# Chunk inverses of a delta rule: doublings on 32-row diagonal blocks in place of 64-row blocks

## The chip, the core and the metric

One NeuronCore of a Trainium2 chip runs the whole program in one launch. Its engines work side by side, each through its own instructions in order: TensorE (PE) multiplies matrices from SBUF into PSUM, VectorE (DVE) and ScalarE (ACT) do elementwise work and read PSUM back, GpSimd (POOL) does a little, and SyncE (SP) issues most DMAs. The metric is the device time of one execution in microseconds; lower is better. Times of before are the median of three runs.

## The reference, cut to what matters

A small network on 256 tokens of width 1024: two mixed attention layers, then two layers of feed-forward, a mixing layer, and feed-forward again. The change sits in the mixing layer, in its generalized delta rule of eight heads of 64:

```python
def rwkv7_scan(r, w, k, v, a, b):
    def step(state, inp):
        r_t, w_t, k_t, v_t, a_t, b_t = inp
        sa = jnp.einsum('bhvk,bhk->bhv', state, a_t)
        state = (state * w_t[:, :, None, :] + sa[..., None] * b_t[:, :, None, :]
                 + v_t[..., None] * k_t[:, :, None, :])
        return state, jnp.einsum('bhvk,bhk->bhv', state, r_t)
    ...
    _, y = lax.scan(step, state0, xs)
```

Written in chunks of 64 tokens, the steps inside a chunk are a triangular system of 64 unknowns for each head and chunk. The kernel inverts its unit triangular matrix, and the change is in how.

## The kernel before

**Stages.** `network` runs `even`, `odd`, and then twice `ffn`, `mix`, `ffn`. Weights come from HBM as one stream; SyncE loads parts of 128 x 1024 values, ACT casts each to a high part (`whi`, line 117), DVE subtracts for a low part (`wlo`, line 118), and each projection step is three matmuls of 128 x 128 weights on 256 columns (`mm3`, lines 131 to 133; in `proj_n` lines 317 to 319). `fetch_to` runs four parts ahead of the one in use.

**The mixing layer.** `mix` has two units of four heads. For each it makes k, r and v (`project`), `operands`, and `chunks`; then `chain` walks both units over the four chunks, and `retention` follows. The functions are generators, but alone in `together` a generator's yields change nothing. What sets the order on every engine is a scheduler over the whole program, which places an instruction by its estimate of when its inputs are there; so the projection matmuls of unit 1 and of the retention stand between the steps of `chunks`.

**`chunks`.** A unit has 16 matrices of 64 x 64: two heads on the two halves of the 128 partitions, eight (head pair and chunk) along the free axis. The gram matmuls (line 992) give, masked by `gm`, `gb` and `gk`. The inverse of the unit triangular matrix in `gb[:, :, 0:64]` is built by doubling: `xT` starts with the inverse of blocks of two (lines 998, 999, masks `lev[:, 0]` and `eye`), `x` is its transpose (line 1000; DVE's stream transpose works in blocks of 32 x 32). Level s joins blocks of 2^s to blocks of 2^(s+1):

```python
ps = pairs("t1", lambda e, p, n: gb[p, n, 0:64], lambda e, p, n: x[p, n])
nc.vector.tensor_tensor(t1, ps, b8(lev[:, s]), op=OP.mult)
...
ps = pairs("dx", lambda e, p, n: xT[p, n], lambda e, p, n: t1[p, n])
nc.vector.tensor_tensor(x, ps, x, op=OP.add)
nc.vector.transpose(flat(xT), flat(x))
```

`pairs` (line 975) is 16 matmuls of 64 rows by 64 columns, one for each matrix; the two heads lie on different halves of the array. There are five levels, so ten products in a call; the last adds to `xT` itself (line 1044). Beside them run `values` (vt, line 1009 and 1012), `updates` (bt and nbk, lines 1018 and 1021) and `first` (z, line 975 and 1027). `chain` reads `xT` in its u matmuls (line 1068). Two PSUM banks (`inv`) take turns. In the trace the PSUM tile t1 and the SBUF tile t1 are both named "t", and each program matmul of 32-bit operands of this kind gives two records.

Of the kernel before, what the change touches and what calls it, by code (L numbers as in the profile page):

```python
# [9 lines left out]
F32 = mybir.dt.float32  # L10
# [3 lines left out]
OP = mybir.AluOpType  # L14
# [37 lines left out]
class Net:  # L52
# [782 lines left out]
    def mix(self, tag, l, cst):  # L835


        nc, tc, ident = self.nc, self.tc, self.ident
# [3 lines left out]
        with ExitStack() as c:  # L842
            psum = self.banks.using(mm=(0, 1), ch=(2, 4), ss=(3,), inv=(5, 6), y=(7, 3))
            work = c.enter_context(tc.tile_pool(name="mw", bufs=1))

            gm, lev, eye, scan, rot, cos, sin, dec = (cst[n] for n in MIX_CONST)
# [72 lines left out]
            def w8(name, n, bufs=2):  # L919
                return work.tile([128, 8, n], F32, tag=name, name=name, bufs=bufs)  # L920

            c8 = lambda t: t.rearrange("p u (c t) -> p (u c) t", t=C)
            flat = lambda m: m.rearrange("p n t -> p (n t)")
# [47 lines left out]
            def pairs(name, lhs, rhs, tag="inv"):  # L971
                ps = psum.tile([128, 8, 64], F32, tag=tag, name=name)
                for n in range(8):
                    for e, p in enumerate(heads):
                        nc.tensor.matmul(ps[p, n], lhs(e, p, n), rhs(e, p, n), start=True, stop=True)  # L975
                return ps

            def chunks(q, b):


                ar, bk, v = (q[n] for n in ("ar", "bk", "v"))

                gb, gk = w8("gb", 128), w8("gk", 128)
                for u in range(2):
                    yield
                    m = slice(4 * u, 4 * u + 4)
                    pb = psum.tile([128, 4, 128], F32, tag="inv", name="gram")
                    pk = psum.tile([128, 4, 128], F32, tag="inv", name="gram")
                    for n in range(4):
                        for ps, w in ((pb, heads[0]), (pk, heads[1])):  # L990
                            for p in heads:
                                nc.tensor.matmul(ps[p, n], bk[p, 4 * u + n, w], ar[p, 4 * u + n], start=True, stop=True)  # L992
                    for g, ps in ((gb, pb), (gk, pk)):
                        nc.vector.tensor_tensor(g[:, m], ps, gm[:, None, :].to_broadcast([128, 4, 128]), op=OP.mult)

                b8 = lambda m: m[:, None, :].to_broadcast([128, 8, 64])
                x, xT = w8("x", 64, 1), w8("xT", 64)
                nc.vector.tensor_tensor(xT, gb[:, :, 0:64], b8(lev[:, 0]), op=OP.mult)
                nc.vector.tensor_tensor(xT, xT, b8(eye), op=OP.add)
                nc.vector.transpose(flat(x), flat(xT))  # L1000

                vt = work.tile([128, 2, 4, 64], F32, tag="vt", name="vt", bufs=2)
                nbk = work.tile([128, 8, 2, 64], F32, tag="nbk", name="nbk", bufs=2)

                def values():
                    ps = psum.tile([128, 2, 2, 128], F32, tag="inv", name="vt")
                    for u in range(2):
                        for i in range(2):
                            nc.tensor.transpose(ps[:, u, i], v[:, u, 128 * i:128 * i + 128], ident)
                    for i, p in enumerate(heads):  # L1010
                        for e in range(2):
                            nc.scalar.copy(vt[heads[e], :, i::2], ps[p, :, :, heads[e]])

                def updates(u):
                    m = slice(4 * u, 4 * u + 4)
                    ps = psum.tile([128, 4, 128], F32, tag="inv", name="bt")
                    for n in range(4):
                        nc.tensor.transpose(ps[:, n], bk[:, 4 * u + n], ident)
                    for i in range(2):
                        for p in heads:  # L1020
                            nc.scalar.copy(nbk[p, m, i], ps[heads[i], :, p])

                def first():
                    ps = pairs("z0", lambda e, p, n: gk[p, n, 0:64],
                               lambda e, p, n: vt[p, n // 4, n % 4])
                    z0 = q["z0"] = work.tile([128, 2, 4, 64], F32, tag="z0", name="z0", bufs=2)
                    nc.scalar.copy(z0.rearrange("p u n t -> p (u n) t"), ps)

                side = [values, lambda: updates(0), lambda: updates(1), first]
                t1 = w8("t1", 64, 1)  # L1030
                for s in range(1, 6):
                    yield
                    ps = pairs("t1", lambda e, p, n: gb[p, n, 0:64], lambda e, p, n: x[p, n])
                    nc.vector.tensor_tensor(t1, ps, b8(lev[:, s]), op=OP.mult)
                    if side:
                        side.pop(0)()
                    yield
                    if s < 5:
                        ps = pairs("dx", lambda e, p, n: xT[p, n], lambda e, p, n: t1[p, n])
                        nc.vector.tensor_tensor(x, ps, x, op=OP.add)  # L1040
                        nc.vector.transpose(flat(xT), flat(x))
                    else:
                        ps = pairs("dx", lambda e, p, n: t1[p, n], lambda e, p, n: xT[p, n])
                        nc.vector.tensor_tensor(xT, ps, xT, op=OP.add)
                q.update(gb=gb, gk=gk, vt=vt, nbk=nbk, xT=xT)

            def chain(q, b):
# [92 lines left out]
            for name in "krv":  # L1140
                project(name, 0)
            together(operands(units[0], 0))
            together(chunks(units[0], 0))
            for name in "krv":
                project(name, 1)
# [274 lines left out]
def constants():  # L1420

    f = np.float32
    p = np.arange(128)
    c = {}
    c["ident"] = np.eye(128, dtype=f)
    c["e2"] = (p[:, None] // 64 == np.arange(2)[None]).astype(f)
    slopes = np.power(2.0, -np.arange(1, 9)).astype(f)
    t1, t0 = p[:, None] + 128, p[:, None]
    keys = np.concatenate([np.tile(np.arange(256), (128, 1)), np.tile(np.arange(128), (128, 1))], 1)
    dist = np.concatenate([np.tile(t1, 256), np.tile(t0, 128)], 1) - keys  # L1430
    c["dist"] = np.stack([np.where((dist >= 0) & (dist < w), dist, -NEG) for w in (256, 128)], 1).astype(f)
    pairs = [2.0 ** -(4 * e + t + 1) for t in range(4) for e in range(2)]
    sl = np.stack([1 / slopes, slopes, 1 / np.array(pairs), pairs])
    c["slopes"] = np.broadcast_to(sl[None], (128, 4, 8)).astype(f)
    c["blk64"] = (p[:, None] // 64 == p[None] // 64).astype(f)
    tp = p[:, None, None] + 128 * np.arange(2)[None, :, None]
    dc = (tp - (16 * np.arange(15) + 31)[None, None]).astype(f)
    c["cmask"] = (dc >= 0).astype(f)
    cb = np.where(dc[:, :, None] >= 0, -slopes[None, None, :, None] * dc[:, :, None], f(NEG))
    c["cbias"] = cb.astype(f).reshape(128, 16, 15)  # L1440

    s, t = p[:, None] % 64, p[None] % 64
    c["gm"] = np.where(p[None] < 64, s < t, s <= t).astype(f)
    s, t = p[:, None] % 64, np.arange(64)[None]
    lev = [(s // 2 == t // 2) & (s < t)]
    for w in (2, 4, 8, 16, 32):
        lev.append((s // (2 * w) == t // (2 * w)) & (s // w > t // w))
    c["lev"] = np.stack(lev, 1).astype(f)
    c["eye"] = (s == t).astype(f)
    c["scan"] = np.broadcast_to((np.arange(S) % 64 != 0).astype(f)[None], (128, S))  # L1450
    half = p % 64 // 32
    c["rot"] = np.zeros((128, 128), f)
    c["rot"][np.where(half == 0, p + 32, p - 32), p] = np.where(half == 0, f(-1), f(1))
    inv = (f(1.0) / np.power(f(10000.0), np.linspace(0.0, 1.0, 32, dtype=f))).astype(f)
    ang = (inv[p % 32][:, None] * np.arange(S, dtype=f)[None]).astype(f)
    c["cos"], c["sin"] = np.cos(ang).astype(f), np.sin(ang).astype(f)
    i, j = np.arange(S)[None], np.arange(S)[:, None]
    d = np.where(i // 64 == j // 64, np.abs(i - j), np.where(i > j, i - j, np.inf))
    lg = np.log(1.0 - np.power(2.0, -5.0 - np.arange(4)))
    dec = np.exp(lg[:, None, None] * d[None]) * 64 ** -0.5  # L1460
    c["dec"] = dec[:, :128].transpose(1, 0, 2).astype(f)
    c["vmask"] = ((p[:, None] // 15) == np.arange(8)[None]).astype(f)
    return c
# [54 lines left out]
```

## Time and profile before

| what | us |
|---|---|
| median of 3 runs (1466.73 to 1468.81) | 1468.05 |
| the profiled execution | 1467.17 |
| its span, first to last instruction | 1465.4 |
| PE busy (98%) | 1432.1 |
| DVE busy (69%) | 1013.0 |
| ACT busy (50%) | 739.8 |

The page gives each engine's busy time, the chain of work that ended last, and groups of instructions by line. A matmul's row gives its start and a modelled length in which neighbours overlap, so what a matmul costs is read from start to start. The mean granted TensorE clock is 0.991.

### The profile page before, as it was taken

Reading aid. Unit: us, or ns where it says so; the run is one execution under the profiler, and the core shown is the slowest. Engines: PE = TensorE matmul, PEld = TensorE weight load, DVE = VectorE, ACT = ScalarE, POOL = GpSimd, SP = SyncE. Lnnn points to the kernel's source line nnn. Section 1 sums busy time; section 2 is a strip of 40 time slices with the busy share of each in tenths; the row PEclk is TensorE's granted clock in tenths of the full one; section 3 lists DMA queues with packets and bytes.
Section 4 is the critical chain, followed back from the end, with each engine's and each line's share of the span. In section 5 each row is a group of like instructions: output and inputs, shape, how many; then the busy total and the mean of one; then the engine's idle time right before and its main releaser. Section 6 shows DMA issues by size and latency. Waiting matters only on the chain.

```text
span 1465.4 us, 31747 instructions
## 1 busy us (share of the span) xinstructions
PE 1432.1 (98%) x13326; PEld 1370.9 (94%) x13326; DVE 1013.0 (69%) x1804; ACT 739.8 (50%) x1268; POOL 23.9 (2%) x54
## 2 busy tenths in 40 slices
PE   8899989999999999999999999999999999999997
PEld 7699979899999989898999999999998988999997
DVE  7879798886555678657655668556678756765564
ACT  6947555855444474335444445444457324544443
POOL 0000000000000000000000000000000001000000
PEclk9999999999999999999999999999999999999998
DMA  8244534265555534124555555555553213555551
GB/s 297 76 130 132 179 125 144 87 206 177 186 184 184 180 116 129 47 87 122 180 181 182 187 187 173 184 178 187 187 173 116 74 32 101 173 178 183 186 187 44
DMA packets 63600, 222.01 MB, mean 151 GB/s; under 512 B 7744, under 2 KB 9024, under 8 KB 63456
## 3 DMA queue, kind: packets, MB, share of 16 engines
q1 hardware_dynamic: 62928, 219.31, 47.0%
q8 instruction: 104, 1.70, 0.5%
q10 hardware_dynamic: 432, 0.53, 0.1%
q14 instruction: 40, 0.33, 0.1%
q0 software_dynamic: 96, 0.13, 0.0%
HBM read 218.90 MB, written 1.05 MB: 150 GB/s over the span
## 4 chain that ended last, share of the span: by engine, by line
PE 91%; ACT 4%; DVE 3%; issue 1%; POOL 1%; DMA 0%; POOLq 0%; DVEq 0%; ACTq 0%
PE gu L131 11%; PE gu L133 11%; PE gu L132 11%; PE mm L132 6%; PE mm L131 6%; PE mm L133 6%; PE acc L131 6%; PE acc L132 6%; PE acc L133 6%; PE t L975 2%; PE dx L975 1%; PE gram L992 1%; PE gu L282 1%; PE s L370 1%; ACT whi L117 1%
## 5 line engine op out<-in xcount | busy, mean ns | idle before, releaser
L118 DVE TENSOR_TENSOR wlo<-raw,whi 128x1024 fp32r<-128x1024 f32 (+1 forms) x412 | 499.1, 1213 | 209.2 <-ACT whi L117 208.8
L117 ACT CAST whi<-raw 128x1024 fp32r<-128x1024 f32 (+1 forms) x412 | 426.8, 1039 | 416.8 <-PE gu L132 167.4
L131 PE MATMUL gu<-hh,whi 128*128 128x256 f32 x1344 | 380.7, 283 | 0.1
L132 PE MATMUL gu<-hl,whi 128*128 128x256 f32 x1344 | 380.3, 283 | 0.0
L133 PE MATMUL gu<-hh,wlo 128*128 128x256 f32 x1344 | 380.2, 283 | 0.0
L131 PEld LDWEIGHTS gu<-hh,whi 128*128 128x128 f32 x1344 | 257.3, 191 | 0.6 <-issue 0.2
L133 PEld LDWEIGHTS gu<-hh,wlo 128*128 128x128 f32 x1344 | 257.4, 192 | 0.0
L132 PEld LDWEIGHTS gu<-hl,whi 128*128 128x128 f32 x1344 | 257.3, 191 | 0.0
L132 PE MATMUL acc<-ml,whi 128*128 128x256 f32 x704 | 197.6, 281 | 0.0
L133 PE MATMUL acc<-mh,wlo 128*128 128x256 f32 x704 | 197.5, 281 | 0.0
L131 PE MATMUL acc<-mh,whi 128*128 128x256 f32 x704 | 196.9, 282 | 0.1
L131 PE MATMUL mm<-hh,whi 128*128 128x256 f32 x608 | 178.4, 293 | 6.8 <-ACT whi L117 6.5
L132 PE MATMUL mm<-hl,whi 128*128 128x256 f32 x608 | 175.8, 289 | 0.1
L133 PE MATMUL mm<-hh,wlo 128*128 128x256 f32 x608 | 175.6, 289 | 0.0
L132 PEld LDWEIGHTS acc<-ml,whi 128*128 128x128 f32 x704 | 132.7, 189 | 0.0
L131 PEld LDWEIGHTS acc<-mh,whi 128*128 128x128 f32 x704 | 132.0, 189 | 0.7 <-ACT mh L139 0.3
L133 PEld LDWEIGHTS acc<-mh,wlo 128*128 128x128 f32 x704 | 132.5, 188 | 0.0
L131 PEld LDWEIGHTS mm<-hh,whi 128*128 128x128 f32 x608 | 117.1, 193 | 11.3 <-ACT whi L117 6.5
L132 PEld LDWEIGHTS mm<-hl,whi 128*128 128x128 f32 x608 | 117.2, 193 | 2.9 <-issue 1.2
L133 PEld LDWEIGHTS mm<-hh,wlo 128*128 128x128 f32 x608 | 117.0, 192 | 2.2 <-issue 0.9
L257 DVE TENSOR_TENSOR t<-gu,rs 128x512 f32<-128x512 f32 x88 | 60.4, 690 | 54.8 <-PE gu L133 54.8
L139 ACT CAST mh<-g 128x256 fp32r<-128x256 f32 x88 | 35.3, 406 | 100.4 <-DVE g L260 100.4
(396 smaller groups left out, 2210.2 us busy)
## 6 DMA issues: line engine op xcount, KB each, us to landing
raw<-in_stream SPq DMA_DIRECT2D x404, 512.0 KB, 3.5
raw<-in_stream SPq DMA_DIRECT2D x4, 280.0 KB, 2.6
x<-in_x SPq DMA_DIRECT2D x4, 256.0 KB, 5.0
raw<-in_stream SPq DMA_DIRECT2D x4, 256.0 KB, 5.2
lora<-in_lora SPq DMA_DIRECT2D x2, 512.0 KB, 5.1
dec<-in_dec SPq DMA_DIRECT2D x1, 512.0 KB, 5.5
out<-o SPq DMA_DIRECT2D x2, 256.0 KB, 3.0
out<-o ACTq DMA_DIRECT2D x2, 256.0 KB, 2.8
```

Source lines behind the costliest of these rows:

```text
L117: nc.scalar.copy(hi, raw)
L118: nc.vector.tensor_tensor(lo, raw, hi.bitcast(F32), op=OP.subtract)
L131: mm(out, ah, bh, start=start, stop=False, skip_group_check=True)
L132: mm(out, ah, bl, start=False, stop=False, skip_group_check=True)
L133: mm(out, al, bh, start=False, stop=stop, skip_group_check=True)
L139: nc.scalar.copy(hi, src)
L257: nc.vector.tensor_tensor(t, ps, self.rsb, op=OP.mult)
L282: mm(ps[:, u], part, self.h[k][0], start=(i + j == 0), stop=False, skip_group_check=True)
L370: nc.tensor.matmul(ps[:, 0:256], q[p, 128:256], kT[p, :], start=True, stop=True)
L975: nc.tensor.matmul(ps[p, n], lhs(e, p, n), rhs(e, p, n), start=True, stop=True)
L992: nc.tensor.matmul(ps[p, n], bk[p, 4 * u + n, w], ar[p, 4 * u + n], start=True, stop=True)
```

## The change

The first inverse and the doublings up to blocks of 32 work on the two diagonal blocks of 32 x 32 of each matrix alone. Four ACT copies bring those blocks of `gb` side by side (`g`, 32 columns for each matrix); `x` and `xb` (its transpose) have 256 columns in place of 512, and the masks are cut to 32 columns. A product is `blocks`: 32 matmuls of 32 rows by 32 columns on the four diagonal tiles of the array. DVE's multiply, add and transpose work on half the columns. The last doubling has one block of 32 x 32 for each matrix: 16 matmuls for its first product, two ACT copies out of PSUM, 16 matmuls for the second, and ACT copies of the diagonal blocks (four) and of the new block (two) into `xT`, whose remaining block GpSimd has set to zero. `values`, `updates`, `first` and `chain` are the same.

```diff
-                b8 = lambda m: m[:, None, :].to_broadcast([128, 8, 64])
-                x, xT = w8("x", 64, 1), w8("xT", 64)
-                nc.vector.tensor_tensor(xT, gb[:, :, 0:64], b8(lev[:, 0]), op=OP.mult)
-                nc.vector.tensor_tensor(xT, xT, b8(eye), op=OP.add)
-                nc.vector.transpose(flat(x), flat(xT))
+                gx = work.tile([128, 2, 8, 32], F32, tag="x", name="gx")
+                g, x = gx[:, 0], gx[:, 1]
+                tx = work.tile([128, 2, 8, 32], F32, tag="t1", name="tx")
+                t1, xb = tx[:, 0], tx[:, 1]
+                b8 = lambda m: m[:, None, :].to_broadcast([128, 8, 32])
+                rows = [slice(32 * i, 32 * i + 32) for i in range(4)]
+                own = [slice(32 * (i % 2), 32 * (i % 2) + 32) for i in range(4)]
+                xT = w8("xT", 64)
+                for e in range(2):
+                    nc.gpsimd.memset(xT[rows[2 * e + 1], :, 0:32], 0.0)
+                for r, w in zip(rows, own):
+                    nc.scalar.copy(g[r], gb[r, :, w])
+                nc.vector.tensor_tensor(xb, g, b8(lev[:, 0]), op=OP.mult)
+                nc.vector.tensor_tensor(xb, xb, b8(eye), op=OP.add)
+                nc.vector.transpose(flat(x), flat(xb))
...
-                t1 = w8("t1", 64, 1)
-                for s in range(1, 6):
+
+                def blocks(name, lhs, rhs, to=range(4), of=range(4)):
+                    ps = psum.tile([128, 8, 32], F32, tag="inv", name=name)
+                    for n in range(8):
+                        for i, k in zip(to, of):
+                            nc.tensor.matmul(ps[rows[i], n], lhs(rows[k], n), rhs(rows[k], n), start=True, stop=True)
+                    return ps
+
+                for s in range(1, 5):
                     yield
-                    ps = pairs("t1", lambda e, p, n: gb[p, n, 0:64], lambda e, p, n: x[p, n])
+                    ps = blocks("t1", lambda r, n: g[r, n], lambda r, n: x[r, n])
                     nc.vector.tensor_tensor(t1, ps, b8(lev[:, s]), op=OP.mult)
                     if side:
                         side.pop(0)()
                     yield
-                    if s < 5:
-                        ps = pairs("dx", lambda e, p, n: xT[p, n], lambda e, p, n: t1[p, n])
-                        nc.vector.tensor_tensor(x, ps, x, op=OP.add)
-                        nc.vector.transpose(flat(xT), flat(x))
-                    else:
-                        ps = pairs("dx", lambda e, p, n: t1[p, n], lambda e, p, n: xT[p, n])
-                        nc.vector.tensor_tensor(xT, ps, xT, op=OP.add)
+                    ps = blocks("dx", lambda r, n: xb[r, n], lambda r, n: t1[r, n])
+                    nc.vector.tensor_tensor(x, ps, x, op=OP.add)
+                    nc.vector.transpose(flat(xb), flat(x))
+
+                yield
+                ps = blocks("t1", lambda r, n: gb[r, n, 32:64], lambda r, n: x[r, n], (1, 3), (0, 2))
+                for i in (1, 3):
+                    nc.scalar.copy(t1[rows[i]], ps[rows[i]])
+                for i in range(4):
+                    nc.scalar.copy(xT[rows[i], :, own[i]], xb[rows[i]])
+                yield
+                ps = blocks("dx", lambda r, n: t1[r, n], lambda r, n: xb[r, n], (0, 2), (1, 3))
+                for i in (0, 2):
+                    nc.scalar.copy(xT[rows[i], :, 32:64], ps[rows[i]])
...
+    t = s // 32 * 32 + np.arange(32)[None]
     lev = [(s // 2 == t // 2) & (s < t)]
-    for w in (2, 4, 8, 16, 32):
+    for w in (2, 4, 8, 16):
```

The scheduler orders the engines anew. Three places follow, all at the first doubling of unit 0 in layer 0. "mm" rows are projections, t is the first product's PSUM tile, dx the second's; gx holds g and x, tx holds t1 and xb. On PE before, from the last mm ahead of t to dx:

```order
L132 MATMUL mm<-hl_6420,whi 128x256
L975 MATMUL t_6884<-x,gb 64x64 x16
L133 MATMUL mm<-hh_6419,wlo 128x256
L131 MATMUL mm<-hh_6423,whi 128x256
L132 MATMUL mm<-hl_6424,whi 128x256
L133 MATMUL mm<-hh_6423,wlo 128x256
L131 MATMUL mm<-hh_6427,whi 128x256
L132 MATMUL mm<-hl_6428,whi 128x256
L133 MATMUL mm<-hh_6427,wlo 128x256
L131 MATMUL mm<-hh_6431,whi 128x256
L132 MATMUL mm<-hl_6432,whi 128x256
L975 MATMUL dx<-t_6883,xT 64x64 x16
```

And now:

```order
L132 MATMUL mm<-hl_6444,whi 128x256
L1046 MATMUL t_6890<-gx 32x32 x32
L133 MATMUL mm<-hh_6443,wlo 128x256
L131 MATMUL mm<-hh_6447,whi 128x256
L132 MATMUL mm<-hl_6448,whi 128x256
L133 MATMUL mm<-hh_6447,wlo 128x256
L131 MATMUL mm<-hh_6419,whi 128x256
L132 MATMUL mm<-hl_6420,whi 128x256
L1046 MATMUL dx<-tx 32x32 x32
```

t stands six mm earlier in the mm stream (20 in place of 26 after the lora matmuls), and six mm in place of nine stand between t and dx. On DVE the same stretch, from the gram's last read-back to the multiply of t (lines 1034 and 1052), before:

```order
L994 TENSOR_TENSOR gb<-gram,gm 128x512
L118 TENSOR_TENSOR wlo<-raw,whi 128x1024
L998 TENSOR_TENSOR xT<-gb,lev 128x512
L118 TENSOR_TENSOR wlo<-raw,whi 128x1024
L999 TENSOR_TENSOR xT<-xT,eye 128x512
L863 TENSOR_TENSOR pz<-mm,rs 128x2x256
L1000 STREAM_TRANSPOSE x<-xT 128x512
L118 TENSOR_TENSOR wlo<-raw,whi 128x1024
L867 SCALAR_TENSOR_TENSOR pr<-pz,rest,pd 128x256
L1034 TENSOR_TENSOR t_6883<-t_6884,lev 128x512
L867 SCALAR_TENSOR_TENSOR pr<-pz,rest,pd 128x256
```

And now:

```order
L994 TENSOR_TENSOR gb<-gram,gm 128x512
L118 TENSOR_TENSOR wlo<-raw,whi 128x1024 x2
L1009 TENSOR_TENSOR tx<-gx,lev 128x256
L863 TENSOR_TENSOR pz<-mm,rs 128x2x256
L1010 TENSOR_TENSOR tx<-tx,eye 128x256
L1011 STREAM_TRANSPOSE gx<-tx 128x256
L867 SCALAR_TENSOR_TENSOR pr<-pz,rest,pd 128x256 x2
L931 SCALAR_TENSOR_TENSOR lsem<-scan,sw 128x256
L1052 TENSOR_TENSOR tx<-t_6890,lev 128x256
```

Both L867 and the first scan (line 931, which reads sw) stand ahead of the multiply of t. On ACT, which makes pd (line 866) and sw (line 892) for these, before:

```order
L1012 COPY vt<-vt 64x4x64 x4
L117 CAST whi<-raw 128x1024
L889 ACTIVATE sw<-pw,half 128x256
L890 ACTIVATE av<-pa,half 128x256
L889 ACTIVATE sw<-pw,half 128x256
L890 ACTIVATE av<-pa,half 128x256
L892 ACTIVATE sw<-sw 128x512
L892 ACTIVATE av<-av 128x512
L866 ACTIVATE pd<-pz,vec 128x256 x2
```

And now:

```order
L1023 COPY vt<-vt 64x4x64
L1008 COPY gx<-gb 32x256 x4
L1023 COPY vt<-vt 64x4x64 x3
L889 ACTIVATE sw<-pw,half 128x256
L890 ACTIVATE av<-pa,half 128x256
L889 ACTIVATE sw<-pw,half 128x256
L890 ACTIVATE av<-pa,half 128x256
L866 ACTIVATE pd<-pz,vec 128x256 x2
L892 ACTIVATE sw<-sw 128x512
```

The four copies of the diagonal blocks stand among the copies of vt, the weight cast has moved behind, and pd stands ahead of sw.

## Rows read from the trace of the kernel before

**Rows 1.** The page: busy time of each engine, and the chain that ended last.

```profile
PE 1432.1 (98%) x13326; PEld 1370.9 (94%) x13326; DVE 1013.0 (69%) x1804; ACT 739.8 (50%) x1268; POOL 23.9 (2%) x54
...
PE 91%; ACT 4%; DVE 3%; issue 1%; POOL 1%; DMA 0%; POOLq 0%; DVEq 0%; ACTq 0%
```

**Rows 2.** Windows (unit 0, unit 1): PE, PEld, DVE, ACT, POOL busy us (x); clock; DMA.

```profile
548.00:592.00 44.00, 43.72 (x635) 39.43 (x633) 36.76 (x55) 22.18 (x43) 2.03 (x3) 1.00 0.37 115
592.00:637.00 45.00, 44.92 (x915) 40.40 (x913) 28.10 (x53) 9.45 (x19) 0.00 (x0) 1.00 0.13 44
```

**Rows 3.** Groups by line and shape: count, busy us, mean ns, idle before.

```profile
L975 PE MATMUL t<-x,gb 64*64 64x64 f32 x640 | 23.0, 221 | 0.7 <-DVE x L1000 0.3
L975 PE MATMUL dx<-t,xT 64*64 64x64 f32 x512 | 18.3, 221 | 0.0
...
L975 PE MATMUL dx<-xT,t 64*64 64x64 f32 x128 | 4.6, 221 | 0.0
```

**Rows 4.** Timeline of PE (start us, length us): products among mm, unit 0.

```profile
573.66 0.28 PE L132 MATMUL mm<-hl,whi 128*128 128x256 f32 x1
573.87 1.15 PE L975 MATMUL dx<-t,xT 64*64 64x64 f32 x32
574.95 0.39 PE L133 MATMUL mm<-hh,wlo 128*128 128x256 f32 x1
575.17 0.28 PE L131 MATMUL mm<-hh,whi 128*128 128x256 f32 x1
...
576.61 0.28 PE L131 MATMUL mm<-hh,whi 128*128 128x256 f32 x1
577.02 1.15 PE L975 MATMUL t<-x,gb 64*64 64x64 f32 x32
577.97 1.13 PE L975 MATMUL z<-vt,gk 64*64 64x64 f32 x32
578.95 1.15 PE L975 MATMUL dx<-t,xT 64*64 64x64 f32 x32
```

**Rows 5.** Timeline of PE: 32 gram records and the mm that follows.

```profile
551.21 1.96 PE L992 MATMUL gram<-ar,bk 64*64 64x128 f32 x32
553.10 0.39 PE L132 MATMUL mm<-hl,whi 128*128 128x256 f32 x1
```

**Rows 6.** Timeline of PE: the conv's two pairs of tiles.

```profile
39.81 0.38 PE L465 MATMUL own<-hp,dg 64*64 64x256 f32 x2
39.83 0.38 PE L469 MATMUL other<-hs,dg 64*64 64x256 f32 x2
40.03 0.38 PE L465 MATMUL own<-hp,dg 64*64 64x256 f32 x2
```

**Rows 7.** Timeline of ACT, DVE and PE ahead of the first t.

```profile
555.48 1.50 ACT L1012 COPY vt<-vt 64x256 f32<-64x256 f32 x4 [0.24 <-PE vt L1009]
...
558.09 0.47 ACT L889 ACTIVATE sw<-pw,half 128x256 f32<-128x256 f32 x1
559.53 0.65 ACT L892 ACTIVATE sw<-sw 128x512 f32<-128x512 f32 x1
560.57 0.92 ACT L866 ACTIVATE pd<-pz,vec 128x256 f32<-128x256 f32 x2
561.37 1.05 ACT L117 CAST whi<-raw 128x1024 fp32r<-128x1024 f32 x1
...
556.92 0.39 PE L131 MATMUL mm<-hh,whi 128*128 128x256 f32 x1
560.00 0.28 PE L132 MATMUL mm<-hl,whi 128*128 128x256 f32 x1
560.43 1.15 PE L975 MATMUL t<-x,gb 64*64 64x64 f32 x32 [0.16 <-DVE x L1000]
```

**Rows 8.** Groups of DVE by shape: this doubling's multiply, and a 128x256 op.

```profile
L1034 DVE TENSOR_TENSOR t<-t,lev 128x512 f32<-128x512 f32 x20 | 13.7, 686 | 7.4 <-PE t L975 7.4
L260 DVE TENSOR_TENSOR g<-g,t 128x256 f32<-128x256 f32 x88 | 36.6, 420 | 2.5 <-ACT g L259 2.2
```

## Prediction

> **What bounds the kernel now.** I read the page first. TensorE (PE) is busy 98% of the span and the chain that ended last is 91% PE [rows 1], so what the change does to PE's time counts nearly in full, and time on other engines counts only where PE waits for it. Then the stretches around the chunk inverses: in layer 0 they run from 548 to 637 us, PE is busy 88.6 of 89.0 us there at the full granted clock (1.00, the 2.4 GHz level), VectorE (DVE) 64.9 and ScalarE (ACT) 31.6 [rows 2]. PE is dense because the scheduler lays projection matmuls ("mm"; 556.92 to 560.00 are 25 steps of 0.12 us [rows 7]) between the dependent products of the inverse. So the question is how much PE time a product costs, not how long the chain of one inverse is.
>
> The products: each program matmul of 64 rows appears as two records in the trace. The groups of line 975 show 640 records of "t" and 512 + 128 of "dx" [rows 3]: 40 products of 32 records, ten in each of the four calls of `chunks` (two units in each of two layers).
>
> What a product costs: three products (t, z, dx) stand back to back, t to z 0.95 us, z to dx 0.98 [rows 4]. Its 32 records lie on two tiles of the array, one for each head, 16 on each, so a record of 64 columns holds its tile for 0.95 / 16 = 59 ns. The 32 gram records stream 128 columns: 1.89 us until the next mm, of which some 0.10 is the way out of the block, so 1.79 / 16 = 112 ns [rows 5]. With 32-row blocks the columns that stream and those of the weights halve alike.
>
> Do four tiles run at once? The conv of the first layer uses four tiles of 64 rows: every 0.22 us two records of "own" and, 0.02 later, two of "other" start, four of 256 columns [rows 6]. At the slope of the rows above (112 for 128 columns) one such record alone takes some 0.22, so all four tiles stream at once.
>
> **The change, part by part.**
>
> *Matmul time.* 32 of the 40 products (four doublings, two each, four calls) become 32 matmuls of 32 rows, 64 records on four diagonal tiles, again 16 on each. 8 products (the last doubling) become 16 matmuls, 32 records on two tiles, 16 on each. So every product has 16 records a tile and only the columns halve. The trace has no record of 32 columns by 32. Bounds from the rows: if the time is in the columns, the line through 59 ns (64) and 112 ns (128) gives 32.5 ns, 0.52 us a product; if it is a fixed turn-around, 59 ns stays and nothing is won. I take 32.5, since 64 and 128 columns lie nearly in proportion. 40 x (0.95 - 0.52) = **-17.2 us**.
>
> The conv rows also show that a matmul's second record, which waits for its own tile, does not hold up the other tiles. By the Trainium skill ("TensorE: Matmul & The Clock Gate", Part 3, The mechanism), matmuls start and end strictly in program order. By that rule each second record would hold up all behind it and this term would be near 0 in place of -17.2; the conv rows disagree, since four tiles could then not share each 0.22 us.
>
> *Switches.* A block among the mm costs more than its records: 573.66 to 575.17 us holds one dx and two mm steps, 1.51 - 0.95 - 0.24 = 0.32 us [rows 4]. In the order of the instructions the stretches of small-tile matmuls between full-width ones rise from 58 to 70 in the program (the scheduler packs fewer mm between products and splits the last dx in one and fifteen): 12 x 0.32 = +3.8 us. Ten more switches are between 32-row and 64-row matmuls directly; no row has one, between 0 and 0.32; I take 0.1, nearer to the 0 that t, z and dx show at one size: +1.0. Together **+4.8 us**.
>
> *Waits of PE.* Before, DVE's multiply of t stands before the scan of line 931, and PE waits only 0.2 us ahead of t. Now ACT first makes four copies of the diagonal blocks (g), and DVE's first multiply of t is queued behind two L867 and one L931, which wait for ACT. Walk in unit 0: a copy of this size follows the last by 0.375 us (1.50 for four) [rows 7]. The eight copies (four vt, four g) run 555.48 to 558.48; four tanh, 0.36 each, to 559.92; pd twice at 0.40; so sw is done near 561.4, where it was done at 560.2 before, and the cast between them is moved behind. DVE then scans (0.69 at most, as the multiply of line 1034), multiplies from about 562.1 for 0.42 (the mean of a 128x256 op [rows 8]), and dx can start near 562.6. PE has t at 559.6 (20 mm after 556.9), six mm behind it, and is ready at 561.15: a wait of 1.45 us, in each layer: +2.9. After that site my walk finds PE and DVE within 0.2 us of each other, since DVE's three ops a doubling fall from 0.69 to 0.42 [rows 8]. The last doubling replaces two DVE ops by ACT copies: from t to dx two copies and two hand-overs, about 1.2 us, against four mm or two rot: +0.3 a call, +1.2. In unit 1 the chain of unit 0 loses mm cover at one place (z, then u): +0.4 a layer, +0.8. One wait of before (0.2 ahead of t at 577.0 [rows 4]) goes in each layer: -0.4. Together **+4.5 us**; from 0 (if the scans' inputs come earlier than I walk) to 9 (if two sites cost as much).
>
> *At nothing.* DVE loses about 0.27 us on 60 ops (16 us) and eight whole ops, hidden, as DVE is not the bound; where it is late is in the waits above. ACT gains 48 copies of 0.37 (18 us), hidden beside PE in the long run: it has 57 us idle in these 89. The weight casts wait behind them, but the weights are cast some four parts ahead, and a part lasts PE 2.9 us (24 mm). GpSimd's two memsets a call go to xT, read only by the chain: if that cover went, a fraction of a us. Projection work is only moved later, into the long mm run ahead of the retention.
>
> *Sum.* -17.2 + 4.8 + 4.5 = -7.9. Against the profiled execution (1467.17, its span 1465.4 and 1.8 around it) that is 1459.3; it lay 0.9 below the median of 1468.05, so **1460.2 us** (-0.54%) for the median.
>
> **The rivals.**
>
> *Fixed turn-around (slower).* A record of 32 columns holds its tile as long as one of 64. Nothing comes off the products, the switches stay (+4.8), and the waits shrink to about 2, as each product covers 0.4 more: 1468 + 6.8 = 1475. It decides from about 48 ns a record on (40 x 0.17 us is then all that pays for the 6.8). For it: the trace has nothing under 59 ns on a tile. Against: 59 to 112 is almost a doubling.
>
> *Each matmul held up by the second record of the one before (slower).* A doubling product then takes 32 x 32.5 ns = 1.04 us, +0.09 on 32 products and -0.43 on 8, -0.5 in all, with the same switches and waits 1474. Against: the conv rows.
>
> *PE's instruction rate (slower).* The densest row is a product, 32 records (each with its weight load) in 0.95 us, 30 ns each. If that is how fast PE takes instructions, 64 records take 1.9 us: 32 x 0.95 = +30, 8 products unchanged, with switches 1503. For it: nothing denser is sustained. Against: in the conv rows the two pairs of records start 20 ns apart, and the records stand at the halves that the columns explain.
>
> The Trainium skill ("TensorE: Matmul & The Clock Gate", "Wait — 56ns, not 53.3ns?") states a floor of about 25 ns between starts of small matmuls. If that holds over all tiles together, an estimate is 64 x 25 = 1.6 us a product, and the time about 1490; no row here shows whether it does.
>
> *The waits eat it.* The tiles are fast but ACT and DVE hand over late at several sites as at the first; six such waits more of 1.2 us: 1467. For it: DVE is busy 36.8 of 44.0 us beside unit 0 [rows 2]. Against: it gets lighter.
>
> *More than forecast.* The waits do not come: 1455. Part of the forecast's range.
>
> **How the numbers follow.** Two versions differing by under 0.2% (2.9 us) can't be told apart here. Chances: forecast 0.60 (1454 to 1465), waits eat it 0.13 (1465 to 1471), fixed turn-around 0.12 and held-up matmuls 0.03 (1471 to 1477), instruction rate 0.12 (1485 to 1503). The range leaves out the last and the edges: 1454 to 1475. Faster takes the forecast and a little of the second, 0.62; same most of the second, 0.13; slower the rest, 0.25.
>
> **What would show it.** Right: a 32-row product of 64 records from its first start to the next block in about 0.5 to 0.6 us; a wait of PE ahead of the first dx of unit 0, DVE scanning just before it; mm at 0.12 unchanged; mix stages some 4 us shorter each, all else equal. Wrong: records of a tile 50 ns apart or more, 64 records in 0.95 to 1.9 us, the way in or out of a 32-row block well over 0.32 us, or PE waits ahead of most products.

## The result, and the profile after

The changed kernel takes 1480.3 us (median; 1479.0 to 1487.2) against 1467.8 for the kernel before: ratio 1.0095 with an interval of 1.0079 to 1.0111, 12.5 us slower. The forecast was 1460.2, 0.5% faster; the direction was wrong and the time lies outside the range. The runs below show where the forecast gain went: the products did become about as fast as forecast, and TensorE (PE) then ran out of instructions and lost clock. The stops for instructions are shown by experiment; why the clock fell is in part open.

The profiled execution of the changed kernel is its slowest, 1487.15 (span 1485.4). Two lines of its page, the busy times and the queue that brings PE its instructions (packets, MB, share of the DMA engines):

```profile
PE 1438.4 (97%) x14350; PEld 1370.7 (92%) x14350; DVE 994.2 (67%) x1796; ACT 758.0 (51%) x1316; POOL 26.4 (2%) x62
...
q8 instruction: 112, 1.84, 0.5%
```

and the same queue before:

```profile
q8 instruction: 104, 1.70, 0.5%
```

PE has 1024 records and as many weight loads more than before, 2048 instructions; the queue has eight packets more. So a packet of 16.4 KB (1.84 MB / 112) holds 256 PE instructions. That the bursts below stop after every 128 records and their 128 weight loads says the same.

The stages, to be read against [rows 2], where PE was busy 43.7 of 44.0 and 44.9 of 45.0 us at clock 1.00. Columns: the stretch, its length, then busy time of PE, PEld, DVE, ACT and POOL, the granted clock, DMA share and GB/s. The last two stretches are layer 1:

```profile
548.00:592.00 44.00, 39.84 (x866) 33.63 (x866) 30.52 (x53) 25.75 (x55) 2.03 (x3) 0.96 0.30 92
592.00:637.00 45.00, 42.69 (x1147) 36.99 (x1143) 20.99 (x48) 12.94 (x29) 0.00 (x0) 0.92 0.15 45
1121.00:1165.00 44.00, 40.20 (x831) 33.71 (x830) 27.57 (x48) 23.86 (x52) 1.98 (x3) 0.85 0.27 86
1165.00:1217.00 52.00, 47.96 (x1170) 41.72 (x1168) 23.05 (x50) 13.83 (x30) 0.00 (x0) 0.87 0.15 43
```

Two things are new: PE stands idle for 14 us of these 185, and the granted clock is under 1.00 in all four. What PE waited for in layer 0 (line waited for, us in total, times, longest):

```profile
PE t L1046 <- issue: 2.3, 3, 1.4
PE bt L1029 <- issue: 1.6, 1, 1.6
PE dx L1046 <- DVE tx L1052: 1.2, 1, 1.2
PE mm L132 <- issue: 0.7, 1, 0.7
PE dx L1046 <- issue: 0.2, 1, 0.2
PE t L1046 <- DVE gx L1011: 0.2, 1, 0.2
```

and in layer 1:

```profile
PE dx L1046 <- issue: 4.9, 4, 1.6
PE dx L1046 <- DVE tx L1052: 1.2, 1, 1.2
PE t L1046 <- ACT whi L117: 0.9, 1, 0.9
PE t L1046 <- issue: 0.5, 1, 0.5
```

"issue" means that PE waited for nothing that the profile shows. Together these are 10.2 us, and a second profile of the same kernel has 10.4. Before has none there; in the stretch of each layer its one wait is:

```profile
PE t L975 <- DVE x L1000: 0.2, 1, 0.2
```

The DVE wait of 1.2 us is the forecast one. The timeline of PE in layer 0 shows both kinds (start, length, instruction, records, idle time before and its releaser):

```profile
559.99 0.74 PE L1046 MATMUL t<-gx 32*32 32x32 f32 x64 [0.20 <-DVE gx L1011]
562.83 0.75 PE L1046 MATMUL dx<-tx 32*32 32x32 f32 x64 [1.18 <-DVE tx L1052]
...
572.70 0.75 PE L1046 MATMUL dx<-tx 32*32 32x32 f32 x64
574.17 0.64 PE L1046 MATMUL t<-gx 32*32 32x32 f32 x51
576.22 0.32 PE L1046 MATMUL t<-gx 32*32 32x32 f32 x13 [1.41 <-issue]
```

At 574.6 PE stops in the middle of one product, after 51 of its 64 records, and goes on 1.6 us later. A data wait can't do that, since all 64 read the same tile `gx`, which was complete before the first of them. The instruction queue's packets of this stretch start at 569.4, 574.0 and 577.4 and take about 1 us each; PE goes on 1.3 to 1.5 us after each has landed.

### The profile page after: what moved, and what is told of

Read it like the earlier page. It is cut to its first block, busy times and chain, and to the rows that moved or that the text cites. A ratio compares the mean times of both kernels' runs of the same rounds, so it can differ in the third digit from the quotient of the medians.

```text
span 1485.4 us, 33845 instructions
## 1 busy us (share of the span) xinstructions
PE 1438.4 (97%) x14350; PEld 1370.7 (92%) x14350; DVE 994.2 (67%) x1796; ACT 758.0 (51%) x1316; POOL 26.4 (2%) x62
## 3 DMA queue, kind: packets, MB, share of 16 engines
q8 instruction: 112, 1.84, 0.5%
## 4 chain that ended last, share of the span: by engine, by line
PE 90%; ACT 4%; DVE 3%; issue 2%; POOL 1%; DMA 0%; POOLq 0%; DVEq 0%; ACTq 0%
PE gu L131 11%; PE gu L133 11%; PE gu L132 11%; PE mm L132 6%; PE mm L131 6%; PE mm L133 6%; PE acc L131 6%; PE acc L132 6%; PE acc L133 6%; PE dx L1046 1%; PE gu L282 1%; PE gram L992 1%; PE t L1046 1%; PE s L370 1%; ACT whi L117 1%
```

## Experiments

**Half the instructions (e2).** The products of the four doublings:

```diff
+                def halves(name, lhs, rhs):
...
+                    for n in range(4):
+                        for i in range(4):
+                            nc.tensor.matmul(ps[rows[i], 2 * n:2 * n + 2], lhs[rows[i], n], rhs[rows[i], 2 * n:2 * n + 2],
+                                             start=True, stop=True)
...
-                    ps = blocks("t1", lambda r, n: g[r, n], lambda r, n: x[r, n])
+                    ps = halves("t1", g, x)
...
```

> The changed kernel, but each product of the four 32-row doublings is 16 matmuls in place of 32: the weights of matrix n move over the columns of matrices 2n and 2n+1 at once (64 columns), so the second of each pair, and n from 4 on, get the wrong weights and the inverse is not the inverse. Each tile streams the same number of columns, with half the PE instructions. Instruction supply theory: a product has 64 instructions in about 0.5 us, about 117 per us in place of 233; the stops put down to issue (18 us under line 1046 in the changed kernel) shrink below 3 us, the clock comes back to 0.989 or more, time 1455 to 1464. Rival (the 32-row tiles lower the clock): no stops but the clock stays at 0.978 to 0.985, time 1466 to 1474. Rival (the loss is in hand-overs between engines): the waits for DVE and ACT stay and so does the time, 1474 or more.

Measured: 1457.2 us (ratio 0.9921, 0.9901 to 0.9941), clock 0.988 to 0.993. The products, on PE's timeline:

```profile
569.87 0.65 PE L1053 MATMUL t<-gx 32*32 32x64 f32 x32
570.45 1.15 PE L975 MATMUL z<-vt,gk 64*64 64x64 f32 x32
571.53 0.65 PE L1053 MATMUL dx<-tx 32*32 32x64 f32 x32
```

A product takes 0.58 us to the next block, z at 64 rows 1.08. The issue waits in the two chunk stretches fall from 10.2 us (the 18 us of the expectation counts the waits of PE's weight loads a second time) to one:

```profile
PE t L1046 <- issue: 0.4, 1, 0.4
```

So with the same tiles, the same work on DVE and ACT, and half the instructions in these products, the stops are gone and the kernel is as fast as forecast. What it leaves out is the right inverse, since matrices get another's weights, and the order of the engines differs too, since the scheduler estimates it anew. The clock still falls behind unit 0's last doubling in layer 0, while PE has no idle time:

```profile
577.00:585.00 8.00, 8.00 (x38) 6.29 (x38) 4.34 (x8) 2.66 (x5) 1.82 (x1) 0.57 0.21 66
```

**A burst measured by itself (e7, e8).** In the kernel before, behind its last projections, with 32 moved columns (e7, shown) and with 64 (e8):

```diff
...
+        for j in range(128):
+            for i in range(4):
+                r = slice(32 * i, 32 * i + 32)
+                nc.tensor.matmul(pb[r, j % 16], self.x[7][r, 0:32], self.x[7][r, 32:64], start=True, stop=True)
```

> The kernel before with 512 extra matmuls of 32 rows by 32 columns on the four diagonal tiles, in one block behind the last projections (their result is not used). 1024 records and 1024 weight loads, 2048 PE instructions, 8 blocks of 256. Full speed as the 32-row products of the changed kernel show it (64 records in 0.55 us): 8.8 us. Instruction supply theory: after what is fetched ahead, PE stops at every block of 256 instructions, which come every 2.3 to 2.6 us (a fetch of about 1 us and some 1.3 us until PE goes on): 17 to 20 us for the block, with gaps of 1.1 to 1.5 us between groups of about 128 records, time about 1484. Rival (PE runs them at full speed, the stops of the changed kernel came from something else): 8.8 us without gaps over 0.3 us, time about 1476.

> The same 512 extra matmuls of 32 rows, each moving 64 columns in place of 32: the same 2048 PE instructions at half the rate (64 records in about 0.9 us). Full speed 14.4 us. Instruction supply theory: 256 instructions last 1.8 us, less than the 2.3 to 2.6 of a fetch, so the stops stay but shrink to 0.5 to 0.8 us each, and the block takes the same 17 to 20 us as with 32 columns. Rival (no supply limit): 14.4 us without gaps, 6 us more than the block of 32 columns.

Measured: 1495.8 and 1495.9 us, 28.4 and 28.6 more than before, so twice the columns cost nothing here, and both missed the 17 to 20 us expected. PE in the burst of 32 columns:

```profile
1454.25 2.56 PE L1247 MATMUL burst<-x 32*32 32x32 f32 x174
1457.96 1.93 PE L1247 MATMUL burst<-x 32*32 32x32 f32 x128 [1.15 <-issue]
1461.70 1.93 PE L1247 MATMUL burst<-x 32*32 32x32 f32 x128 [1.81 <-issue]
1465.45 1.93 PE L1247 MATMUL burst<-x 32*32 32x32 f32 x128 [1.81 <-issue]
```

and of 64:

```profile
1454.96 6.12 PE L1247 MATMUL burst<-x 32*32 32x64 f32 x302
1462.83 1.99 PE L1247 MATMUL burst<-x 32*32 32x64 f32 x128 [1.76 <-issue]
1466.85 1.99 PE L1247 MATMUL burst<-x 32*32 32x64 f32 x128 [2.03 <-issue]
1470.59 1.99 PE L1247 MATMUL burst<-x 32*32 32x64 f32 x128 [1.76 <-issue]
```

Exactly 128 records (256 instructions) run, then PE stops for 1.2 to 2.1 us: mostly 3.74 us from group to group in the one, 3.5 to 4.0 in the other. This is the supply: 256 instructions in some 3.75 us, slower than the 2.3 to 2.6 that I expected. The packets show why: each takes 0.9 to 1.4 us, but starts only when about two thirds of the block before it has run (1459.1 in the group that starts at 1457.96, 1462.9 in the next), and PE goes on 1.2 to 1.6 us after it has landed. The blocks of both bursts ran in about the same time (1.7 and 1.8 us from first to last start), because the narrow one ran at half the clock, as shown next; the supply of blocks that run faster was not measured by itself. In the doublings of layer 0 the changed kernel's packets start 3.4 to 5.1 us apart, near that limit, and before they are 5.6 to 11.6 apart. In layer 1 before has one pair 3.4 apart, without a stop.

The clock differs: the burst of 32 columns ran at the lower level (0.50, 1.2 GHz) from end to end, that of 64 at the full one from 1458.4 us on, with stops as long:

```profile
1454.00:1482.00 28.00, 15.69 (x1028) 14.65 (x1028) 0.00 (x0) 2.08 (x6) 0.00 (x0) 0.50 0.02 5
```

```profile
1459.00:1482.00 23.00, 12.46 (x817) 11.51 (x811) 0.00 (x0) 0.00 (x0) 0.00 (x0) 1.00 0.02 4
```

So stops alone, here of 1.5 to 2.0 us, do not lower the clock. In both bursts it fell at the first record (1454.2 and 1455.0), behind 22 matmuls of one moved column and before any stop. With 64 columns it rose again within the first group, which ran 6.1 us without a stop; with 32 the first stop came after 2.6 us and it stayed low. Whether the columns or the longer run made the difference is not separated.

**As many instructions, slower (e3).** The kernel before, each doubling matmul split in two of 32 columns:

```diff
...
+                    for h in (slice(0, 32), slice(32, 64)):
+                        for e, p in enumerate(heads):
+                            nc.tensor.matmul(ps[p, n, h], lhs(e, p, n), rhs(e, p, n)[:, h], start=True, stop=True)
```

> The kernel before, with 64-row tiles, but each matmul of the first four doublings is split in two of 32 columns with the same weights: as many PE instructions as the changed kernel, at about half its rate (128 in some 1.0 us). Instruction supply theory with a rate limit: the rate is near what a fetch of 256 instructions in about 2.4 us can give (107 per us), so a few stops, shorter than 0.7 us; the work of TensorE grows by 32 x about 0.1 = 3 us; time 1469 to 1476, clock 0.987 or more if the clock fell because of stops over 1 us. Rival (the number of instructions or fetches counts, not the rate): the loss of the changed kernel, 18 us of issue, clock 0.985 or less, 1482 or more. Rival (nothing but the 32-row tiles matters): no stop, clock 0.991, 1470 to 1472.

Measured: 1500.8 us (1.0223, 1.0208 to 1.0238), clock 0.989 to 0.993. 112 packets as in the changed kernel, and no stop: the one wait of PE in layer 0's stretch is 0.2 us for DVE, and the waits of layer 1 are for ACT and DVE. So the rate counts, not the number. The time missed my range, and the reason is a finding:

```profile
564.17 2.06 PE L983 MATMUL dx<-t,xT 64*64 64x32 f32 x64
567.42 2.06 PE L983 MATMUL t<-x,gb 64*64 64x32 f32 x64
```

64 records last 1.84 us from first to last start, 58 ns a record on each of two tiles, as much as with 64 moved columns [rows 3, 4]. With weights of 64 columns a record holds its tile 58 ns even when half as much moves. 32 x (1.84 - 0.93) = 29 of the 33.6 us lost, with 0.93 us for a product of before from first to last start.

**Without the copies of the blocks (e4).** DVE forms the first inverse from `gb` in four slices:

```diff
-                for r, w in zip(rows, own):
-                    nc.scalar.copy(g[r], gb[r, :, w])
-                nc.vector.tensor_tensor(xb, g, b8(lev[:, 0]), op=OP.mult)
+                for r, w in zip(rows, own):
+                    nc.vector.tensor_tensor(xb[r], gb[r, :, w], lev[r, 0][:, None, :].to_broadcast([32, 8, 32]), op=OP.mult)
...
```

> The changed kernel without the four ACT copies of the diagonal blocks: the first products read the blocks where the gram left them, and VectorE forms the first inverse with four multiplies on 32 partitions each. As many PE instructions as the changed kernel. Instruction supply theory: the wait of 1.46 us ahead of the first dx of unit 0 goes or shrinks (up to -2.9 us over the two layers), the issue stops and the clock below 0.987 stay: 1474 to 1482. Rival (the hand-over waits are the loss): 1470 or less. If VectorE's four small multiplies cost more than the copies: 1480 to 1486 with PE waiting for DVE at the first product.

Measured: 1481.0 us (1.0095, 1.0078 to 1.0112), clock 0.981 to 0.986. PE's waits in layer 0:

```profile
PE t L1045 <- issue: 2.1, 4, 0.7
PE dx L1045 <- issue: 1.7, 1, 1.7
...
PE bt L1028 <- issue: 0.8, 1, 0.8
PE t L1045 <- DVE gx L1010: 0.6, 1, 0.6
...
PE dx L1045 <- DVE tx L1051: 0.5, 1, 0.5
```

The wait of 1.2 us ahead of the first dx is replaced by two of 0.6 and 0.5, and the time is the changed kernel's. Hand-overs are not the loss.

**The last doubling alone (e1), and with 64 moved columns (e10).**

The second product of e1; its first, with two ACT copies, is changed alike:

```diff
-                        ps = pairs("dx", lambda e, p, n: t1[p, n], lambda e, p, n: xT[p, n])
-                        nc.vector.tensor_tensor(xT, ps, xT, op=OP.add)
...
+                ps = blocks("dx", lambda r, n: t1[r, n, 0:32], lambda r, n: xT[r, n, 32:64], (0, 2), (1, 3))
+                for i in (0, 2):
+                    nc.scalar.copy(xT[rows[i], :, 32:64], ps[rows[i]])
```

> Before's 64-row doublings are kept; only the last doubling is done on its one 32-row block (16 + 16 matmuls, the ACT copies of the result). It has as many PE instructions as before. Instruction supply theory (TensorE ran out of instructions because 64-record products of 0.55 us use them up faster than they are fetched, and the clock fell behind those stops): no idle PE time put down to issue over 0.5 us in the two chunk stretches, clock as before (0.991), and the saving of the last doubling alone, 8 products x 0.43 = 3.4 us, less up to 1.2 for the ACT hand-overs: 1464 to 1467. Rival (matmuls of 32 rows lower the granted clock by themselves): clock below 0.990 with half clock near the last doublings, 1468 or more. Rival (ACT hand-overs are dear): 1468 to 1472 at full clock, with PE waiting for ACT.

> The kernel with only the last doubling on one 32-row block (1469.9, with half clock for 3.4 us behind the last doubling of unit 0 in each layer), but its matmuls move 64 columns in place of 32 (the other 32 are not used). Same instructions, same hand-overs, 8 products longer by 0.4 us (+3.4). If matmuls of 32 columns let the clock fall there: the half clock behind unit 0's last doubling is gone (0.991 or more), up to 3.4 us come back, 1468 to 1471. If the hand-overs or the order let it fall: half clock stays and the time is 1472 to 1474.

Measured: e1 1469.9 us (1.0014, 1.0005 to 1.0023), e10 1476.8 (1.0072, 1.0053 to 1.0090). In e1 a product takes 0.50 + 0.12 us where it took 0.91 + 0.15, 3.5 us less on eight, and there is no stop. Yet e1 lies above the 1464 to 1467 expected, where the rival with the clock put it. Behind unit 0's last doubling the clock falls, which it did not before (there 1.00 over 583 to 592). In e1:

```profile
583.00:592.00 9.00, 9.00 (x82) 6.99 (x81) 3.84 (x8) 3.06 (x8) 1.81 (x1) 0.81 0.21 60
```

In layer 1 it is 0.81 too. So the clock can fall with no stop near. In e10 this stretch is at 1.00 again in layer 0 but still 0.81 in layer 1, and the time rose by 6.9 where the columns explain 3.4: neither reading of it holds fully, and what lets the clock fall there stays open. The mean clock of e10's executions, 0.984 to 0.988 against 0.989 to 0.991 in e1, says that it lost clock in other places.

**A version with fewer instructions for the same result (e6, e9, e11).** The inverse of the 32-row blocks as (I + L)(I + L^2)(I + L^4)(I + L^8)(I + L^16): the weights P serve P P and P X in one matmul of 64 columns, five products in place of eight. Weights `g` hold the transpose of P; `px` holds P beside X:

```diff
...
+                for s in range(5):
+                    yield
+                    w = slice(0, 1) if s == 0 else slice(0, 2) if s < 4 else slice(1, 2)
+                    ps = power(g, w)
+                    if s < 4:
+                        nc.vector.transpose(flat(g), flat(ps[:, 0]))
+                        nc.scalar.copy(px[:, 0], ps[:, 0])
+                    if s:
+                        nc.vector.tensor_tensor(x, ps[:, 1], x, op=OP.add)
...
```

In e9 the side work starts one product later (`if s: side.pop(0)()`); in e11 the last doubling also moves 64 columns.

> The inverse of the diagonal blocks of 32 by powers in place of masked doublings: with L the strictly triangular block, X = (I + L)(I + L^2)(I + L^4)(I + L^8)(I + L^16). The weights P = L^(2^k) serve both P P and P X, so one matmul moves 64 columns (P beside X), and a call has 5 products of 128 PE instructions (first and last with 32 columns) in place of 8; the last doubling as in the changed kernel. Instruction supply theory: a middle product has 128 instructions in about 0.9 to 1.0 us and three fewer blocks follow each other, so the stops put down to issue are gone or under 3 us in all, the clock is 0.988 or more; matmul time of a call 2 x 0.56 + 3 x 0.95 + 2 x 0.56 = 5.1 us against 9.5 before, 4 x 4.4 = 17.6 off, plus switches and waits of about 5 to 8: 1452 to 1461, faster than both kernels. Rival (what was lost lies in waits of the doublings' chain, which is shorter here too): also faster, but with waits for DVE and ACT in place of issue. Rival (32-row tiles lower the clock): clock 0.985 or less and 1465 or more.

> The kernel by powers (1462.3), with the side work (values, updates, first) started one product later, so that the vt and nbk copies of ScalarE no longer stand between the first product and its read-back, where TensorE waited 0.9 us for vt and 0.4 for nbk in each layer. If those waits are what is left: 1458 to 1461. If they only move to the later products or the chain, 1461 to 1465. Instruction stops none in either case.

> The kernel by powers with its side work late (1461.4, half clock for 6.8 us behind unit 0's last doubling in each layer), with the last doubling's matmuls moving 64 columns in place of 32 (half of them not used): +3.4 us of matmul time. If 32 columns let the clock fall: clock 0.992 in nearly all executions, up to 6.8 us come back, 1457 to 1461, faster than both kernels by more than any so far. If not: the half clock stays, 1463 to 1466.

Measured: e6 1462.3 us (0.9969, 0.9959 to 0.9978), e9 1461.4 (0.9948, 0.9934 to 0.9962), e11 1464.5 (0.9978, 0.9969 to 0.9987). All beat both kernels, if by 0.2 to 0.5%; e9 is the best of them. e6 lies just above the 1452 to 1461 expected. What PE waits for in e9's layer 0 is mostly hand-overs again:

```profile
PE z L975 <- ACT nbk L1031: 0.8, 1, 0.8
PE spread L903 <- ACT wide L899: 0.6, 2, 0.3
PE bt L1028 <- ACT nbk L1031: 0.6, 1, 0.6
PE pw L1052 <- DVE px L1063: 0.5, 2, 0.3
PE pw L1052 <- DVE px L1009: 0.5, 1, 0.5
PE pw L1052 <- issue: 0.4, 1, 0.4
```

e9 still loses clock behind unit 0's last doubling (0.66 over 577 to 587 us); its executions at a mean clock of 0.992 took 1457.3 and 1457.5, the one at 0.986 1464.9. In e11 that stretch is at 1.00 in layer 0, 0.83 in layer 1, and the longer products ate what came back. The powers of L may be less safe numerically than masked doublings for inputs with large entries; that was not explored.

**The changed kernel again (after_again).**

> The changed kernel once more, unedited, with more executions beside the kernel before on this chip: 1479 to 1487, clock 0.978 to 0.986 where before has 0.991 to 0.993. If the clock carries part of the loss, executions with a lower clock are the longer ones, by about 1400 x the difference of clock.

Measured: 1481.1 us (1.0090, 1.0077 to 1.0103). Executions of this kernel at clock 0.978 took 1487.2, at 0.982 1482.9, at 0.984 to 0.986 1478.7 to 1482.4. A line through all eight gives about 1 us for each thousandth, where a program wholly bound by PE would lose 1.48.

## Why the prediction was wrong, by its steps

- **What bounds the kernel: "what the change does to PE's time counts nearly in full, and time on other engines counts only where PE waits for it".** This is the step that failed. PE still bounds the kernel, but the sum priced only PE's matmuls and its waits for data, and put at nothing, without a reason, the supply of its instructions and the granted clock. The runs showed 10.2 us of stops for instructions in their place, and a mean clock down from 0.991 to 0.984 or 0.985. The page of before holds the instruction queue as a line. What twice the records in half the time would ask of it was only a rival (0.12), and that was priced from the spacing of records and not from the queue.
- **Matmul time, -17.2.** Right in mechanism. The 64 records span 0.56 us from first to last start, where 0.52 was forecast: 32 x 0.39 + 8 x 0.43 = -16. The argument that columns moved and columns of weights halve alike was needed: e3 shows that halving the moved columns alone brings nothing. By the Trainium skill ("TensorE: Matmul & The Clock Gate", "Wait — 56ns, not 53.3ns?") small matmuls start some 25 ns apart at least. Over four tiles together they start some 9 ns apart here, so the estimate of 1490 falls; [rows 6] already had two pairs 20 ns apart, which the prediction did not hold against it.
- **Switches, +4.8.** A product among mm costs 567.57 - 566.44 = 1.13 us in the trace of after, for itself (0.56) and two mm steps (0.24): 0.33 more, where 0.32 was taken. The number of stretches was read from the order.
- **Waits, +4.5.** The wait ahead of the first dx is there in both layers and for the reason forecast: DVE's two L867 wait for ACT's pd, and the scan follows before the multiply. PE stands idle for 1.2 us, 1.45 forecast. The others (last doubling, unit 1's chain) do not show among PE's waits, so this term is +2.4.
- **At nothing.** Right but for one place: ACT is 18.2 us busier and DVE 18.8 less (18 and 16 forecast). In layer 1 PE waits 0.9 us ahead of a t, by the profile for ACT's weight cast, which the prediction held to be far enough ahead. The second profile has no such wait, and an instruction packet had landed 1.3 us before PE went on, as at the other stops; which of the two it was stays open.
- **Not in the sum: instruction stops, +10.** 10.2 and 10.4 us in two profiles. By the bursts PE gets 256 instructions in some 3.75 us when it asks for more than that; two 32-row products use up 256 in 1.1 us of work, and the scheduler lays them with fewer mm between.
- **Not in the sum: the clock, +7 to +10.** The sum took 1.00 in these stages because before had it. The mean fell from 0.991 to 0.984 or 0.985 in the usual execution; 7 thousandths are 7 us at the slope of the eight executions and 10 at 1.48. In the profiled one (0.978) they are 13 to 19. There four of the five falls in the chunk stretches come behind a stop of some 1.5 us, as at 1151.7 behind the stop of 1148.5:

```profile
1148.00:1152.00 4.00, 2.51 (x109) 2.16 (x105) 0.87 (x2) 0.59 (x1) 0.00 (x0) 0.96 0.02 6
1152.00:1165.00 13.00, 13.00 (x87) 10.09 (x84) 3.60 (x7) 5.53 (x12) 1.81 (x1) 0.50 0.01 1
```

  Behind it PE worked for 13 us at half clock. The fifth (585.1) has only a stop of 0.5 us ahead of it, and the stop at 574.6 had no fall behind it. That the stops are part of the cause is likely (e2, almost without them, has 0.988 to 0.993), but not shown apart from the narrow products: e1 and e2 lose clock without a stop near, and e8 keeps it with stops.
- **The sum.** -16 + 4.8 + 2.4 + 10.3 and 7 to 10 make +8.5 to +11.5 against +12.5 measured; 1 to 4 us are left without a place. Without the last two terms it is -8.8. That e2 measured -10 is close to this partly by luck: three of its four executions also ran below before's clock, and the one at 0.993 took 1452.3, some 15 us less than before.
- **The rivals.** "PE's instruction rate" (0.12) was nearest and had the wrong form: it priced a steady 30 ns a record, where products run at full speed until a block of 256 is used up. Fixed turn-around is refuted for 32-row tiles, and true for a weight load of 64 columns (e3). Held-up matmuls and late hand-overs are refuted (0.56 us a product; e4). Against held-up matmuls the prediction cites the conv rows; they show that four tiles work at once, but not in which order a matmul's two records were issued, so they do not test program order itself.

By the Trainium skill ("Runtime: NRT & Kernel Launch", "Instruction fetch mechanics") instructions come in blocks of 256 by a queue of their own, ahead of use, at a cost that is mostly hidden. The block size agrees with the trace; that the cost is hidden holds in the kernel before and in e3, and not in the changed kernel and the bursts, where it left stops of up to 2.2 us.

## What to carry to other kernels

Cutting matmuls into smaller tiles trades columns for instructions: count PE instructions (two for each record, with its weight load) per microsecond in the densest stretch, and where 256 of them take less than about 3.5 us (the groups of e7 and e8 came 3.5 to 4.0 us apart), expect stops that no data wait explains. "issue" among PE's waits, inside a block of equal matmuls, is the sign. Share the weights between two products and move both in one matmul before making tiles smaller; and do not carry a granted clock of 1.00 over to a stage whose work you thin out.

## What the runs showed of the hardware that I had not expected

- In a block of equal small matmuls PE got 256 instructions every 3.5 to 4.0 us, with 32 moved columns at half clock and with 64 at full clock alike (e7, e8).
- In the shapes run here, the wider of weights and moved columns set how long a record held its tile: 31.5 ns for 32 by 32; 56 ns for weights of 32 and 64 moved (e2: 32 records in 0.435 us from first to last start, 8 on a tile); 58 ns for weights of 64 and 32 moved (e3); 59 ns for 64 by 64.
- Stops of 1.5 to 2.0 us left the clock at its full level in e8, and in e1 and e2 it fell with no stop near.
